# A gate of a decoder layer by seven products of quarters, its combined weights by adding DMAs, its products summed in the PSUM banks

## The chip, the cores and the metric

The kernel runs on one core of a Trainium2 chip. A core has TensorE (PE, matmuls), VectorE (DVE), ScalarE (ACT), GpSimd (POOL), SyncE (SP, which here only issues DMAs) and 16 DMA engines between the chip's memory (HBM) and the core's on-chip memory (SBUF). Matmuls write into PSUM, of which the kernel uses eight banks. The metric is the time of one execution on the device in microseconds (us).

## The reference, cut to what matters

One decoder layer on 512 tokens of 1024 features, fp32. With `u = rmsnorm(x)`, one wide product gives everything that the token mixer needs:

```
proj = u @ w_in                      # 512 x 1024 times 1024 x 10128
q, k, v, pool_in, z, xbc, dt_raw, gate_pre = split(proj)
y_a = dilated_attention(q, k, v) @ w_a        # 3 groups of 6 heads
y_b = pool_mixer(pool_in) @ w_b
y_c = ssd_mixer(z, xbc, dt_raw) @ w_c
gates = sigmoid(gate_pre + b_gate)            # 3 gates of 1024
x = x + (gates0 * y_a + gates1 * y_b + gates2 * y_c) @ w_o
x = x + conv_ffn(rmsnorm(x))
return rmsnorm(x)
```

The change is about the second gate (`gates1`, 1024 columns of `w_in`), about the columns of V for the attention groups 1 and 2 (384 each), and about those of Q and K for group 1 (384 each).

## The kernel before, in words

**Products.** Every fp32 factor is split into a high and a low part, and a product is three matmuls: high x high, high x low, low x high (`mm3`, L229; the matmul is L237, and in it the parts with the low weights come last). `u` lies in SBUF as `uh` and `ul`, with features on the partitions. A `Job` is one tile of weights: its raw tile is loaded by SP (`fetch`, L183), ScalarE copies it to the high part in two halves (`cast`, L196), VectorE subtracts to get the low part (`low`, L216), and TensorE multiplies (the job's body). High parts have three buffers, low parts two, raw tiles two.

**Order.** The program is a list of jobs with calls between them (`program`, L1504 to L1565). PE, ACT, DVE and POOL run their instructions in the order in which the program writes them; SP's are placed by the scheduler as soon as their buffers allow. At the start of job n the main loop writes: the low part of job n+1, then (if that job has one) its `then`, the cast of n+2 (put on a list, `second`, that is worked off at the job's last `step()` and behind its body), the load of n+3, and then the body of n. A `step()` also moves on the side works (`running`, `waiting`), attention above all, by one piece.

**Plain groups.** `gate_jobs(b)` makes a gate of eight chunks of 128 features: each has 24 matmuls of 512 columns into one bank, a sigmoid on ScalarE (L1226), and for gate 1 a product with the branch's output on VectorE (L1228). Two chunks are a job with a raw tile of 1 MB.

**Groups of seven.** A product of a 2 x 2 matrix of quarters by another such takes eight products of quarters, or seven of combined quarters (a scheme of Strassen's kind). `sums_of_u` (L403) makes the four combined quarters of `u` (VectorE and ScalarE); `side_u` hands out a quarter or a combination. `sevens` (L344) is such a group for V of groups 1 and 2, `qk_sevens` (L700) for Q and K of group 1: seven jobs of quarters of 768 KB. Four quarters of weights are loaded (two by `fetch`, two into tiles `w3` of the pool `ypool`, which has two buffers), and VectorE makes the combined ones by differences in place (`diff`, L341; each runs behind a low part). Each product has two banks of its own; partial results are copied out by ScalarE (L370, L735) and summed by VectorE (L375, L378, L383, L662, L745).

**The stretch.** The order is: pool input jobs, V and Q, K of group 0, attention of group 0 (as side work), the eight chunks of `w_b` with all four `sums_of_u` from its third job on, four chunks of gate 1, the seven products of V, the seven of Q and K, attention of group 1 (side work), the other four chunks of gate 1, twelve chunks of XBC (whose convolution is done behind each), the state-space part, and so on to the FFN, which has two groups of seven of its own (`down_group`) and ends with the norm.

**Other buffers.** General tiles of 2 KB per partition come from the pool `big` with NBIG = 54 buffers. The row of norm factors (`grow`, L444) has a pool of its own (4 KB per partition).

Of the kernel before, what the change touches and what calls it, by code (L numbers as in the profile page):

```python
# [82 lines left out]
def trunk(ctx: ExitStack, tc, out, x, rel_bias, ln1_g, w_in, b_gate, w_a, pool_w, pool_scale, w_b,  # L83
# [10 lines left out]
    rows = ctx.enter_context(tc.tile_pool(name="rows", bufs=1))  # L94
# [5 lines left out]
    ypool = ctx.enter_context(tc.tile_pool(name="ypool", bufs=2))  # L100
# [221 lines left out]
    def sums_of(f0, f1, ah, al, found):  # L322


        sa, sb = T("sa"), T("sb")
        dve.tensor_tensor(sa[:, LO], f0[:, HI], f1[:, HI], OP.add)
        dve.tensor_tensor(sa[:, HI], sa[:, LO], f0[:, LO], OP.subtract)
        dve.tensor_tensor(sb[:, LO], f0[:, LO], f0[:, HI], OP.subtract)
        dve.tensor_tensor(sb[:, HI], f1[:, LO], sa[:, HI], OP.subtract)
# [13 lines left out]

    def sevens(quarter, c, side, W, emit):  # L344

        r1, r2, r3, r5 = {}, {}, {}, {}

        def job(j, load, form, use):  # L350
            def body(ws):
                wh, wl = ws
                parts = side(j)
                for i in range(2):
                    ps = MM("pb")
                    o = slice(i * P, (i + 1) * P)
                    mm3(ps[:, :c], lambda k: wh[:, k, :], lambda k: wl[:, k, :],
                        lambda k: parts[k][0][:, o], lambda k: parts[k][1][:, o], range(4), flip=True)
                    use(i, ps[:, :c])
                step()  # L360
            new = Job([load] if load is not None else [], 4, c, body)
            new.form = form
            if load is None:
                new.load = lambda: None
            return new

        def keep(r, name):
            def use(i, ps):
                r[i] = T(name)[:, :c]
                act.copy(r[i], ps)  # L370
            return use

        def p5(i, ps):
            keep(r5, "r5")(i, ps)
            dve.tensor_tensor(r2[i], r2[i], ps, OP.add)  # L375

        def p6(i, ps):
            dve.tensor_tensor(r1[i], r1[i], ps, OP.add)  # L378
            emit(0, 1, i, r1[i], r2[i])

        def p7(i, ps):
            r3[i] = T("r3")[:, :c]
            dve.tensor_tensor(r3[i], r1[i], ps, OP.add)  # L383
            emit(1, 1, i, r3[i], r5[i])

        one = job("A11", quarter(0, 0), None, keep(r1, "r1"))
        two = job("A12", quarter(1, 0), None, lambda i, ps: emit(0, 0, i, r1[i], ps))
        three = job(4, None, lambda: W[1], keep(r2, "r2"))
        one.then = lambda: diff(one.raw, W[0], one.raw)
        three.then = lambda: diff(W[0], W[1], W[0])  # L390
        two.then = lambda: diff(W[1], W[1], one.raw)
        yield one
        yield three
        yield two
        yield job(1, None, lambda: one.raw, p5)
        yield job(2, None, lambda: W[1], p6)
        yield job(3, None, lambda: W[0], p7)
        yield job("A22", None, lambda: diff(two.raw, two.raw, W[1]),
                  lambda i, ps: emit(1, 0, i, r3[i], ps))
# [3 lines left out]
    def sums_of_u(p):  # L403

        f = []
        for k in (2 * p, 2 * p + 1):
# [4 lines left out]
                           lambda j, h, l: US.__setitem__((j, p), (h, l)))  # L411
# [32 lines left out]
    def grow(src):  # L444
        g = rows.tile([P, D], F32, name="grow", tag="grow")
        sp.dma_start(g, src.partition_broadcast(P))
        return g
# [11 lines left out]
    def norm_early(t, g):  # L459
# [4 lines left out]
        pool.tensor_tensor(xg, t, g[:, :S], OP.mult)  # L464
# [3 lines left out]
    def norm_late(t, g, v0, outs, last=None):  # L468
# [6 lines left out]
        dve.tensor_tensor(xg, t, g[:, S:], OP.mult)  # L475
# [171 lines left out]
    def v_pair():  # L647

        c, W = C_V + 384, []
        vd = dram.tile([S, 384], F32, name="vdram")  # L650
        rows_ = lambda c0: w_in[:, c0:c0 + 384].rearrange("(k two p) c -> two p k c", two=2, p=P)
        quarter = lambda two, h: rows_(c + 384 * h)[two]

        def load():
            for two in range(2):
                W.append(ypool.tile([P, 4, S], F32, name="w3", tag="xs")[:, :, :384])
                sp.dma_start(W[two], quarter(two, 1))

        def emit(hi, right, i, a, ps):
            g, tb = 1 + right, 2 * hi + i  # L660
            t = T(f"v{g}")
            dve.tensor_tensor(t[:, :384], a, ps, OP.add)  # L662
            if g == 2:
                sp.dma_start(vd[tb * P:(tb + 1) * P, :], t[:, :384])
                return

            for n in range(4):
                if (g, n) not in V:
                    V[g, n] = T(f"vr{g}")
                sp.dma_start(V[g, n][32 * tb:32 * tb + 32, :384], t[n:P:4, :384])  # L670
# [8 lines left out]
        return load, sevens(quarter, 384, side_u, W, emit), residues  # L679
# [20 lines left out]
    def qk_sevens(g):  # L700


        W = []
# [3 lines left out]
        r1, r2, r3, r5 = {}, {}, {}, {}  # L707

        def load():
            for two in range(2):  # L710
                W.append(ypool.tile([P, 4, S], F32, name="w3", tag="xs")[:, :, :384])
                sp.dma_start(W[two], quarter(two, 1))

        def job(j, raw, form, use):
            def body(ws):
                wh, wl = ws
                parts = side_u(j)
                for i, ms in enumerate(chunks):
                    ps = MM("pq")
                    for n, m in enumerate(ms):  # L720
                        o = slice(m * P, (m + 1) * P)
                        mm3(ps[:, 256 * n:256 * n + 256], lambda k: wh[:, k, o], lambda k: wl[:, k, o],
                            lambda k: parts[k][0], lambda k: parts[k][1], range(4))
                    use(i, ps[:, :256 * len(ms)])
                step()
            new = Job([raw] if raw is not None else [], 4, 384, body)
            new.form = form
            if raw is None:
                new.load = lambda: None
            return new  # L730

        def keep(r):
            def use(i, ps):
                r[i] = T("rq")[:, :ps.shape[-1]]
                act.copy(r[i], ps)  # L735
            return use

        def emit(which, hi, i, a, b):

            for n, m in enumerate(chunks[i]):  # L740
                if (which, g, m) not in QK:
                    QK[which, g, m] = T(f"{which}{g}")
                view = (grouped if which == "q" else plain)(QK[which, g, m], g)
                piece = lambda t: perm(t[:, 256 * n:256 * n + 256], g)
                dve.tensor_tensor(view[:, :, 64 * hi:64 * hi + 64], piece(a), piece(b), OP.add)  # L745

        def p5(i, ps):
            keep(r5)(i, ps)
            dve.tensor_tensor(r2[i], r2[i], ps, OP.add)

        def later(i):
            emit("k", 0, i, r1[i], r2[i])
# [3 lines left out]
        def p6(i, ps):  # L756
            dve.tensor_tensor(r1[i], r1[i], ps, OP.add)
            running.append(after(1, later(i)))

        def p7(i, ps):  # L760
            r3[i] = T("rq")[:, :ps.shape[-1]]
            dve.tensor_tensor(r3[i], r1[i], ps, OP.add)
            emit("k", 1, i, r3[i], r5[i])

        one = job("A11", quarter(0, 0), None, keep(r1))
        two = job("A12", quarter(1, 0), None, lambda i, ps: emit("q", 0, i, r1[i], ps))
        three = job(4, None, lambda: W[1], keep(r2))
        one.then = lambda: diff(one.raw, W[0], one.raw)
        three.then = lambda: diff(W[0], W[1], W[0])
        two.then = lambda: diff(W[1], W[1], one.raw)  # L770
        return load, [one, three, two, job(1, None, lambda: one.raw, p5), job(2, None, lambda: W[1], p6),
                      job(3, None, lambda: W[0], p7), job("A22", None, lambda: diff(two.raw, two.raw, W[1]),
                                                          lambda i, ps: emit("q", 1, i, r3[i], ps))]

# [729 lines left out]
    def program():  # L1504
        yield from jobs_a(w_in, C_POOL, 8, uhk, ulk, KD, pool_evac)
        yield Call(lambda: waiting.append(rows_of_bias()))
        yield from v_jobs(0)
        yield from qk_jobs(0)
        yield from pool_out_job()
        yield Call(lambda: attend(0))  # L1510
        yield Call(lambda: waiting.insert(3, ssd_prep()))
        for i, job in enumerate(branch_jobs(1, w_b, YB, 8, more=range(7))):
# [3 lines left out]
        load, pair, residues_of_v = v_pair()  # L1516
        yield Call(load)
        yield from gate_jobs(1, 0, SPLIT)
# [267 lines left out]
```

## Time and profile before

| what | value |
|---|---|
| three runs | 1023.89 to 1024.44 us, median 1024.22 |
| the profiled execution | 1024.13 us |
| its span in the profile | 1022.4 us |
| granted TensorE clock | 0.999 |
| bytes moved | 118.08 MB, 115 GB/s over the span |

The profile is of one execution; its own time is 1.73 us more than its span. In the lines below, L237 is a line of the kernel, `pa`, `pb`, `pq` are names of PSUM tiles (`pa` a chunk of a gate, of XBC, of w_b; `pb` V; `pq` Q and K of group 1), `wh` and `wl` high and low parts of weights, `raw` and `w` raw weights. "x24" is a count. A group's row gives the total in us and the mean of one in ns, and then how long the engine was idle just before and what ended that.

### The profile page before, as it was taken

The numbers are of one execution on the slowest core, as the hardware profiler recorded it, in microseconds if no ns is written. First come the engines' busy times: TensorE is split into PE (matmuls) and PEld (weight loads), VectorE is DVE, ScalarE is ACT, GpSimd is POOL, SyncE is SP. The second block draws the span as 40 slices with busy tenths as digits, with TensorE's granted clock in tenths as the row PEclk, the third lists the DMA queues.
The fourth block names the chain that finished last, engine by engine and source line by source line (L and its number), as shares of the span: only waits on it lengthen the run. The fifth ranks groups of instructions, "written<-read, shape, count | busy, mean of one in ns | idle before, by whom it ended". The sixth has DMA issues, their size and how long they took to land.

```text
span 1022.4 us, 13249 instructions
## 1 busy us (share of the span) xinstructions
PE 1013.1 (99%) x5258; PEld 857.6 (84%) x5258; DVE 701.4 (69%) x890; ACT 507.9 (50%) x847; POOL 127.2 (12%) x108
## 2 busy tenths in 40 slices
PE   8999999999999999999999999999999999999997
PEld 8998878899888888888888888898888888888886
DVE  6563566788766656676879666768778768685756
ACT  5432545454574366878567224554444434433434
POOL 1770000000000000000044501102111100111002
PEclk9999999999999999999999999999999999999999
DMA  8444312124442354552254526542232333321322
GB/s 269 138 118 135 105 62 76 31 83 145 124 118 83 87 151 112 145 138 74 79 140 160 165 83 237 178 142 86 94 113 83 99 107 122 126 83 42 124 83 82
DMA packets 114077, 118.08 MB, mean 115 GB/s; under 512 B 6212, under 2 KB 97927, under 8 KB 114016
## 3 DMA queue, kind: packets, MB, share of 16 engines
q1 hardware_dynamic: 113423, 116.39, 37.0%
q8 instruction: 41, 0.67, 0.3%
q10 hardware_dynamic: 592, 0.86, 0.3%
q14 instruction: 21, 0.16, 0.1%
HBM read 113.44 MB, written 3.00 MB: 114 GB/s over the span
## 4 chain that ended last, share of the span: by engine, by line
PE 98%; DMA 1%; DVE 0%; ACT 0%; ACTq 0%; issue 0%
PE pa L237 36%; PE pu L237 22%; PE pb L237 12%; PE pd L237 7%; PE pqk L237 6%; PE pq L237 3%; PE pa L1633 2%; PE ps L799 1%; PE pu L1434 1%; PE ppw L237 1%; PE po L847 1%; PE pt L833 1%; PE py L1132 1%; DMA xin<-in_x_dram 1%; PE pyo L1139 1%; PE pst L1120 0%
## 5 line engine op out<-in xcount | busy, mean ns | idle before, releaser
L216 DVE TENSOR_TENSOR wl<-raw,wh 128x2048 fp32r<-128x2048 f32 (+3 forms) x95 | 220.1, 2318 | 47.5 <-ACT wh L196 39.7
L196 ACT CAST wh<-raw 128x1024 fp32r<-128x1024 f32 (+4 forms) x187 | 186.5, 1017 | 42.7 <-DVE raw L341 18.0
L1329 DVE SCALAR_TENSOR_TENSOR hc<-pu,fcol,hc 128x510 f32<-128x510 f32 x88 | 65.9, 748 | 56.4 <-ACT hc L1326 54.8
L237 PE MATMUL pa<-uh,wh 128*128 128x512 f32 x384 | 97.0, 395 | 0.0
L237 PE MATMUL pa<-ul,wh 128*128 128x512 f32 x384 | 94.9, 389 | 0.0
L237 PE MATMUL pa<-uh,wl 128*128 128x512 f32 x384 | 94.8, 389 | 0.0
L237 PEld LDWEIGHTS pa<-ul,wh 128*128 128x128 f32 x384 | 72.1, 188 | 15.1
L237 PEld LDWEIGHTS pa<-uh,wl 128*128 128x128 f32 x384 | 72.1, 188 | 14.9
L237 PE MATMUL pu<-uh,wh 128*128 128x512 f32 (+1 forms) x352 | 83.5, 379 | 0.0
L237 PE MATMUL pu<-uh,wl 128*128 128x512 f32 (+1 forms) x352 | 83.5, 379 | 0.0
L237 PE MATMUL pu<-ul,wh 128*128 128x512 f32 (+1 forms) x352 | 83.5, 379 | 0.0
L237 PEld LDWEIGHTS pa<-uh,wh 128*128 128x128 f32 x384 | 70.6, 188 | 14.3
L237 PEld LDWEIGHTS pu<-uh,wl 128*128 128x128 f32 x352 | 64.2, 188 | 12.5
L237 PEld LDWEIGHTS pu<-ul,wh 128*128 128x128 f32 x352 | 64.2, 188 | 12.4
L237 PEld LDWEIGHTS pu<-uh,wh 128*128 128x128 f32 x352 | 64.1, 188 | 12.4
L1326 ACT ACTIVATE hc<-pu,fcol,fcol 128x512 f32<-128x512 f32 x40 | 31.2, 779 | 78.9 <-PE pu L237 78.9
L1334 POOL TENSOR_TENSOR hc<-hc 128x512 f32<-128x512 f32 x22 | 30.8, 1401 | 289.0 <-DVE hc L1329 252.0
L1115 POOL TENSOR_TENSOR st<-st,dts 128x512 f32<-128x512 f32 x4 | 4.5, 1126 | 380.4 <-ACT st L1123 322.0
L821 ACT ACTIVATE sb<-sb,nmls 128x128 f32<-128x128 f32 (+1 forms) x72 | 30.0, 418 | 25.7 <-DVE nmls L818 13.6
L1331 ACT ACTIVATE hc<-hc 128x512 f32<-128x512 f32 x22 | 13.9, 632 | 39.9 <-DVE hc L1329 39.9
L1226 ACT ACTIVATE sg<-pa,col 128x512 f32<-128x512 f32 x24 | 16.5, 689 | 32.1 <-PE pa L237 31.0
L969 DVE SCALAR_TENSOR_TENSOR xs<-pa,col,xs 128x509 f32<-128x509 f32 (+2 forms) x24 | 18.0, 749 | 17.1 <-ACT xs L965 16.6
(393 smaller groups left out, 1872.6 us busy)
## 6 DMA issues: line engine op xcount, KB each, us to landing
raw<-in_w_in_dram SPq DMA_DIRECT2D x25, 1024.0 KB, 5.2
raw<-in_ffn_w_up_dram SPq DMA_DIRECT2D x22, 1024.0 KB, 5.1
raw<-in_w_o_dram SPq DMA_DIRECT2D x8, 1024.0 KB
raw<-in_ffn_w_down_dram SPq DMA_DIRECT2D x8, 1024.0 KB, 5.1
raw<-in_w_in_dram SPq DMA_DIRECT2D x14, 512.0 KB, 4.8
raw<-in_w_in_dram SPq DMA_DIRECT2D x6, 768.0 KB, 4.6
raw<-in_w_b_dram SPq DMA_DIRECT2D x4, 1024.0 KB, 5.1
al<-ad SPq DMA_DIRECT2D x16, 256.0 KB, 7.3
```

The lines of the kernel that those rows point to most:

```text
L196: (other.tensor_copy if other and i else act.copy)(job.high[:, :, o], job.raw[:, :, o])
L216: (eng or dve).tensor_tensor(l[:, :, o], job.raw[:, :, o], h[:, :, o].bitcast(F32), OP.subtract)
L237: pe.matmul(ps, l, r, start=first and n == 0, stop=last and n == total - 1, skip_group_check=onto)
L799: pe.matmul(pss[i][:, o:o + w * P], q[r, n * P:(n + 1) * P], k[r, kb * P:(kb + w) * P], start=True, stop=True)
L821: act.activation(sb[:, off:off + w * P], sb[:, off:off + w * P], AF.Exp, bias=nm[:, n, h:h + 1], accum_out=ls[:, n, h:h + 1])
L969: dve.scalar_tensor_tensor(t[:, sh:], ps[:, :S - sh], col[:, o_cw + 12 * k + m:o_cw + 12 * k + m + 1], t[:, sh:], OP.mult, OP.add)
L1226: act.activation(s, ps, AF.Sigmoid, bias=col[:, o:o + 1])
L1326: act.activation(t, ps, AF.Identity, bias=ff["c1"][:, ff["b"] + m:ff["b"] + m + 1], scale=fw(2, m))
L1329: dve.scalar_tensor_tensor(t[:, sh:], ps[:, :S - sh], fw(k, m), t[:, sh:], OP.mult, OP.add)
L1331: act.activation(t, t, AF.Silu)
L1334: pool.tensor_tensor(a, a, t, OP.mult)
L1633: pe.matmul(first[2 * n + j][:, lo:hi], a[:, k, j * P:(j + 1) * P], b[:, k, lo:hi], start=a is wh and b is uh and k == 0, stop=a is wl and ...
```

## The change

1. *The second gate by seven products.* `gate_jobs(1)` is replaced by `gate_seven(1)`: four quarters of 512 x 512 weights (1 MB each), seven products, each of four chunks of 128 features by 256 tokens. Its seven stand in front of those of V. `SPLIT` goes.
2. *One class for the three groups.* `Seven` replaces `sevens` and the body of `qk_sevens`. Order of a group: two, (the last product, four, of the group before), five, three, one, six, seven; four follows behind the next group's two, or behind the first XBC job.
3. *Combined weights by adding DMAs.* Two tiles W0 and W1 per group are loaded by SP. `plus` adds another quarter onto one of them by two DMAs from GpSimd (`accum_op=OP.add`), each of two of the four blocks of 128 rows: 512 KB in the gate, 384 KB in the others. There are four `plus` per group: one after the load (W0), and one behind the low part of five (W0), of three (W1) and of six (W0). VectorE's differences in these groups go.
4. *Products add up in their banks.* Three adds onto the two banks of five; six, seven and four onto those of one. After each product its banks are read: copied out by ScalarE (two, five, three), or added to or subtracted from a kept copy by VectorE (one, six, seven), or read as they are (four). In the gate, a sigmoid on ScalarE follows for each chunk of 256 columns, and a product with the branch's output on VectorE.
5. *Signs.* The scheme needs another sign in one combination of `u` (`turned`).
6. *Places.* `sums_of_u`: two of the four in the Q, K jobs of group 0, two from the third w_b job on. The gate's first tile is loaded ahead of the second w_b job, its second ahead of the third. Attention of group 1 begins behind the first XBC job and Q, K's four.
7. *Memory.* `ypool` three buffers for two, `big` 52 for 54; the row of norm factors is two tiles of `big`, and its pool goes.

The diff, cut to its core:

```diff
+    class Seven:
+        def __init__(self, quarter, c, widths, product, done, name):
+            R, A, B, W = {}, [], [], [None, None]
+            def tile_of(i):
+                W[i] = ypool.tile([P, 4, S], F32, name="w3", tag="xs")[:, :, :c]
+                sp.dma_start(W[i], quarter(i, 1))
+            def plus(i, two, h):
+                for k in (0, 2):
+                    pool.dma_start(W[i][:, k:k + 2, :], quarter(two, h)[:, k:k + 2, :], accum_op=OP.add)
+            def job(j, raw, form, bank, use, more=False):
+                def body(ws):
+                    if not more:
+                        bank[:] = [MM(name) for _ in range(2)]
+                    for i in range(2):
+                        product(bank[i], ws, side_u(j), i, more)
+                        use(i, bank[i][:, :widths[i]])
+                    step()
...
+            self.two = job("A12", quarter(1, 0), None, B, keep(0, 0))
+            five = job(1, None, lambda: W[0], B, keep(1, 1))
+            three = job(4, None, lambda: W[1], B, keep(0, 1), True)
+            one = job("A11", quarter(0, 0), None, A, end(0, 0, OP.add))
+            six = job(2, None, lambda: W[0], A, end(0, 1, OP.subtract), True)
+            seven = job(3, None, lambda: W[1], A, end(1, 1, OP.subtract), True)
+            self.four = job("A22", None, lambda: W[0], A, end(1, 0), True)
+            five.then = lambda: plus(0, 1, 1)
+            three.then = lambda: plus(1, 0, 1)
+            six.then = lambda: plus(0, 1, 0)
+            self.jobs = five, three, one, six, seven
+            self.load = lambda: tile_of(0), lambda: plus(0, 0, 0), lambda: tile_of(1)
...
+    def by_features(chunks):
+        def product(ps, ws, parts, i, more):
+            for n, m in enumerate(chunks[i]):
+                o = slice(m * P, (m + 1) * P)
+                mm3(ps[:, 256 * n:256 * n + 256], lambda k: ws[0][:, k, o], lambda k: ws[1][:, k, o],
+                    lambda k: parts[k][0], lambda k: parts[k][1], range(4), onto=more or n > 0)
+        return product
...
+    def gate_seven(b):
...
+        def done(hi, right, i, r, ps, op):
+            if r is not None:
+                dve.tensor_tensor(r, r, ps, op)
+            for n, m in enumerate(chunks[i]):
+                m += 4 * right
...
+                act.activation(SG[b, m][:, 256 * hi:256 * hi + 256],
+                               (ps if r is None else r)[:, 256 * n:256 * n + 256],
+                               AF.Sigmoid, bias=col[:, o:o + 1])
+                if hi:
+                    running.append(after(1, total(m)))
...
-            if i == 3:
-                yield Call(lambda: running.extend(after(p, sums_of_u(p)) for p in range(4)))
+            if i == 1:
+                yield Call(gates.load[0])
+            if i == 2:
+                yield Call(lambda: running.extend(after(2 * p - 4, sums_of_u(p)) for p in (2, 3)))
+                yield Call(gates.load[1])
+                yield Call(gates.load[2])
             yield job
...
+        last = None
+        for group, next_ in zip(groups, groups[1:] + (None,)):
+            yield group.two
+            if last:
+                yield last.four
+            last = group
+            for i, job in enumerate(group.jobs):
+                if next_ and i >= 2:
+                    yield Call(next_.load[i - 2])
+                yield job
+        xbc = jobs_a(w_in, C_XBC, 12, uhk, ulk, KD, xbc_evac)
+        yield next(xbc)
+        yield last.four
         yield Call(lambda: attend(1))
```

More of the change, by code (lines that the diff above doesn't have):

```diff
@@ L342, in diff @@
         return out
[L344 to L399, printed above, removed]
@@ new lines, in trunk, with keep, use, end @@
+    class Seven:
[15 more added lines that the diff above has]
+                    step()
+                new = Job([raw] if raw is not None else [], 4, c, body)
+                new.form = form
+                if raw is None:
+                    new.load = lambda: None
+                return new
+            def keep(hi, right):
+                def use(i, ps):
+                    r = R[hi, right, i] = T("r7")[:, :widths[i]]
+                    act.copy(r, ps)
+                return use
+            def end(hi, right, op=None):
+                return lambda i, ps: done(hi, right, i, R.get((hi, right, i)), ps, op)
+            self.two = job("A12", quarter(1, 0), None, B, keep(0, 0))
[10 more added lines that the diff above has]
+            self.load = lambda: tile_of(0), lambda: plus(0, 0, 0), lambda: tile_of(1)
@@ L647, in v_pair @@
     def v_pair():
-        c, W = C_V + 384, []
+        c = C_V + 384
         vd = dram.tile([S, 384], F32, name="vdram")
[L651 to L659, printed above, removed]
-            g, tb = 1 + right, 2 * hi + i
-            t = T(f"v{g}")
-            dve.tensor_tensor(t[:, :384], a, ps, OP.add)
+        def product(ps, ws, parts, i, more):
+            o = slice(i * P, (i + 1) * P)
+            mm3(ps[:, :384], lambda k: ws[0][:, k, :], lambda k: ws[1][:, k, :],
+                lambda k: parts[k][0][:, o], lambda k: parts[k][1][:, o], range(4), flip=True, onto=more)
+        def done(hi, right, i, r, ps, op):
+            g, tb = 1 + right, 2 * hi + i
+            if r is None:
+                r = T(f"v{g}")[:, :384]
+                act.copy(r, ps)
+            else:
+                dve.tensor_tensor(r, r, ps, op)
             if g == 2:
-                sp.dma_start(vd[tb * P:(tb + 1) * P, :], t[:, :384])
+                sp.dma_start(vd[tb * P:(tb + 1) * P, :], r)
                 return
@@ L706, in qk_sevens, with done @@
         chunks = ((0, 1), (2,))
[L707 to L738, printed above, removed]
+        def done(hi, right, i, r, ps, op):
+            which = "qk"[right]
             for n, m in enumerate(chunks[i]):
@@ L742, in emit @@
                     QK[which, g, m] = T(f"{which}{g}")
-                view = (grouped if which == "q" else plain)(QK[which, g, m], g)
+                view = (plain if right else grouped)(QK[which, g, m], g)[:, :, 64 * hi:64 * hi + 64]
                 piece = lambda t: perm(t[:, 256 * n:256 * n + 256], g)
[L745 to L749, printed above, removed]
@@ L751, in later, with total @@
-        def later(i):
-            emit("k", 0, i, r1[i], r2[i])
+                if r is None:
+                    dve.tensor_copy(view, piece(ps))
+                else:
+                    dve.tensor_tensor(view, piece(r), piece(ps), op)
+        return Seven(quarter, 384, (512, 256), by_features(chunks), done, "pq")
+    def gate_seven(b):
+        quarter = lambda two, h: w_in[:, C_GATE + b * D + S * h:C_GATE + b * D + S * h + S].rearrange(
+            "(k two p) c -> two p k c", two=2, p=P)[two]
+        chunks = ((0, 1), (2, 3))
+        def total(m):
+            dve.tensor_tensor(MG[m], MG[m], SG[b, m], OP.mult)
@@ L753, in later @@
             return
             yield
[L756 to L773, printed above, removed]
+        def done(hi, right, i, r, ps, op):
+            if r is not None:
+                dve.tensor_tensor(r, r, ps, op)
+            for n, m in enumerate(chunks[i]):
+                m += 4 * right
+                if (b, m) not in SG:
+                    SG[b, m] = T("sg")
+                o = o_bg + 8 * b + m
+                act.activation(SG[b, m][:, 256 * hi:256 * hi + 256],
[3 more added lines that the diff above has]
+                    running.append(after(1, total(m)))
@@ L775, in attend @@
+        return Seven(quarter, S, (512, 512), by_features(chunks), done, "pa")
     def attend(g):
```

48 lines of the change are left out of this document (22 added, 26 removed).

## The prediction

> **What bounds the kernel now.** First the page's totals and its chain of waits, to see which engine sets the end.
>
> ```profile
> span 1022.4 us, 13249 instructions
> PE 1013.1 (99%) x5258; PEld 857.6 (84%) x5258; DVE 701.4 (69%) x890; ACT 507.9 (50%) x847; POOL 127.2 (12%) x108
> PE 98%; DMA 1%; DVE 0%; ACT 0%; ACTq 0%; issue 0%
> ```
>
> TensorE works in 99% of the span and 98% of the chain is TensorE. So time falls only where matmul time falls, and any moment for which TensorE waits is added in full. Next the pieces of the chain around the change (start, length, what; both in us).
>
> ```profile
> 188.44 16.34 PE pa L237 x72
> 204.77 29.14 PE pb L237 x168
> 233.92 30.23 PE pq L237 x252
> 264.15 5.46 PE pa L237 x24
> 270.71 11.11 PE pa L237 x48
> 323.29 38.10 PE pa L237 x168
> ```
>
> The first and the fourth and fifth are gate chunks (24 matmuls of 512 columns each), the last is XBC, `pb` is the second and third V, `pq` is Q and K of group 1. Between these stand only pieces of attention: no gap. The table by stretches (PE, PEld, DVE, ACT, POOL busy; granted clock; share of the DMA engines; GB/s) shows what is free beside them:
>
> ```profile
> 20.00:30.00 10.00, 9.86 (x85) 9.69 (x84) 5.75 (x16) 4.02 (x10) 0.00 (x0) 1.00 1.07 369
> 204.80:233.90 29.10, 29.10 (x170) 29.10 (x170) 24.52 (x25) 13.53 (x21) 0.00 (x0) 1.00 0.39 117
> 233.90:264.10 30.20, 30.20 (x254) 30.20 (x253) 26.22 (x28) 13.48 (x20) 0.00 (x0) 1.00 0.34 110
> ```
>
> In both groups of seven the clock is full, VectorE is busy for 84 to 87%, GpSimd does nothing, and the DMA engines are two thirds idle. Now the groups of operations, shapes kept apart, from 125 to 290 us (busy us, mean ns of one):
>
> ```profile
> L216 DVE TENSOR_TENSOR wl<-raw,wh 128x2048 fp32r<-128x2048 f32 x7 | 16.0, 2283 | 1.0 <-ACT sb L821 1.0
> L196 ACT CAST wh<-raw 128x1024 fp32r<-128x1024 f32 x14 | 14.5, 1046 | 7.0 <-DMA raw<-in_w_in_dram 7.0
> L216 DVE TENSOR_TENSOR wl<-w,wh 128x1536 fp32r<-128x1536 f32 x6 | 10.5, 1753 | 2.0 <-ACT wh L196 2.0
> L196 ACT CAST wh<-w 128x768 fp32r<-128x768 f32 x12 | 9.5, 832 | 3.6 <-DMA w<-in_w_in_dram 3.6
> L1226 ACT ACTIVATE sg<-pa,col 128x512 f32<-128x512 f32 x8 | 5.5, 689 | 15.6 <-PE pa L237 15.5
> L1228 DVE TENSOR_TENSOR yo<-yo,sg 128x512 f32<-128x512 f32 x7 | 4.8, 692 | 15.6 <-ACT sg L1226 15.5
> L341 DVE TENSOR_TENSOR w<-w,w 128x1536 f32<-128x1536 f32 x2 | 3.5, 1753 | 0.0
> L745 DVE TENSOR_TENSOR q<-rq,pq 128x256 f32<-128x256 f32 x6 | 3.3, 608 | 0.0
> L370 ACT COPY r<-pb 128x384 f32<-128x384 f32 x6 | 2.9, 482 | 8.4 <-PE pb L237 8.3
> L735 ACT COPY rq<-pq 128x512 f32<-128x512 f32 x3 | 1.8, 588 | 6.6 <-PE pq L237 6.6
> L735 ACT COPY rq<-pq 128x256 f32<-128x256 f32 x3 | 1.1, 373 | 2.6 <-PE pq L237 2.6
> L375 DVE TENSOR_TENSOR r<-r,pb 128x384 f32<-128x384 f32 x2 | 1.1, 554 | 1.8 <-ACT r L370 1.8
> L326 DVE TENSOR_TENSOR sa<-uf 128x256 f32<-128x256 f32 x4 | 1.7, 418 | 0.0
> ```
>
> and the page's DMA issues (KB each, us from issue to landing); none was issued by GpSimd, none adds:
>
> ```profile
> raw<-in_w_in_dram SPq DMA_DIRECT2D x25, 1024.0 KB, 5.2
> raw<-in_w_in_dram SPq DMA_DIRECT2D x6, 768.0 KB, 4.6
> al<-ad SPq DMA_DIRECT2D x16, 256.0 KB, 7.3
> ```
>
> **The change, part by part.**
>
> 1. *Matmuls of the gate.* Removed are 8 chunks; three of them took 16.34, so one 5.45 and eight 43.57. Added are 7 products of 48 matmuls of 256 columns. The `pq` piece has that shape: 30.23 / 252 = 0.120 each, 336 of them 40.31 (5.76 a product). TensorE saves **3.26 us**. V and the Q, K group keep 168 and 252 matmuls: 0. A product there lasts 29.14 / 7 = 4.16 and 30.23 / 7 = 4.32. This is the only gain that I find, and so about its ceiling.
>
> 2. *Products that add up in their banks.* Before, every product had a bank of its own. Now three adds onto five's bank, and six, seven and four follow one another in one's. The next product cannot begin until the copy or sum of the partial result in its first bank has been read. That read stands in VectorE's or ScalarE's order behind the preparation of a later job, and so does this chain arise: end of product n, evacuation of its second bank, cast of n+2 (ScalarE, two halves), low part of n+2 (VectorE), evacuation of n+1's first bank, start of n+2. It has the length of product n+1 to hide in. Handovers between engines, estimated from this piece of the timeline (cast 209.37 + 1.57 = 210.94, VectorE starts at 210.98), are 0.04 to 0.06; four make 0.2.
>
> ```profile
> 209.37 1.57 ACT L196 CAST wh<-raw 128x768 fp32r<-128x768 f32 x2
> 210.98 1.76 DVE L216 TENSOR_TENSOR wl<-raw,wh 128x1536 fp32r<-128x1536 f32 x1 [0.21 <-ACT wh L196]
> ```
>
>  - Gate, before six: copy 0.59 + cast 2.09 + low 2.28 + sum 0.69 + 0.2 = 5.85 against 5.76: 0.1.
>  - Gate, before seven: sum 0.69, then two sigmoids of 256 columns. No row has that form; 0.373 (the copy of 256) is a lower and 0.689 (the sigmoid of 512) an upper bound, and scaled as the copies are, 0.689 x 373 / 588 = 0.44. 0.69 + 0.87 + 2.09 + 2.28 + 0.69 + 0.2 = 6.82 against 5.86 (product six and the 0.1 before it): 1.0.
>  - Gate's four stands behind V's first product, of 4.16, and needs its low part 8 matmuls (0.96) after its own start: 0.69 + 0.87 + 2.09 + 2.28 + 0.2 = 6.13 against 5.12: 1.0.
>  - V, before six: copy 0.48 + cast 1.66 + low 1.75 + sum 0.55 + 0.2 = 4.64 against 4.16: 0.5.
>  - Q, K, before six: copy 0.37 + 1.66 + 1.75 + two pieces of q at 0.61 + 0.2 = 5.20 against 4.32: 0.9; if a piece costs 0.42, as the plain sums of 256 columns do (L326), 0.5. I take 0.6.
>  - The others have time: before seven of V, ScalarE has nothing to evacuate after product one, so the cast is early.
>
>  Together **3.2** (2.8 to 3.5). With every row a little shorter beside idle neighbours it could be 1.3; below nothing it cannot be, since none of these waits is in the kernel before.
>
> 3. *Weights combined by adding DMAs.* Removed from VectorE: 8 differences of 1.75, 14 us in the two groups, and some of the sums. None of it was on the chain, so it gains 0; it makes the chains of part 2 no worse. Added: 24 adding transfers on GpSimd's queue, in pairs of 384 KB (V, Q and K) or 512 KB (gate). What is queued behind them on GpSimd: nothing but each other, by the zeros of the table. Each pair is issued when the low part of the tile's former use is done, and must have landed at the cast of its next use. From the product lengths: the low part of five is done some 4 us into gate's four, so the pair for V's six has 1.8 + 2 x 4.16 = 10.1; that for seven is issued about 2.2 into five and has 3 x 4.16 - 2.2 = 10.3; that for four has 8.4, and then 2 more, since its own job stands one product further off. So each has **about 10 us**; in the gate 12.8 to 16.
>  What one costs, no row shows. Lower bound: the plain 768 KB, 4.6. Upper bound, far off: `al` at 7.3 for 256 KB, 21.9 for 768. Adding means reading the old tile and the new quarter, so I reckon with up to twice the plain one, 9.2, and take 7: in time, 0. The DMA engines have room for that: four pairs of 768 KB in V's 29.1 us are 108 GB/s, by the first row of the table (1.07 at 369) a share of 0.31, so 0.39 becomes 0.70; at half the rate it becomes 1.01, just full. If the cover is gone, each microsecond over 10 is paid up to six times (six, seven, four, in two groups).
>
> 4. *What is moved.* Two of the four sums of u go to the Q, K jobs of group 0 and two to the w_b jobs: same work, VectorE has room in both, 0; not more than 1 if it hasn't. Attention of group 1 now runs beside the XBC jobs alone instead of four gate chunks and XBC; TensorE's work is the same and XBC lasts to 323.29 + 38.10 = 361.39: 0. At the start, SP issues 0.72 MB more ahead of the third weight tile; at 369 GB/s that is 2 us later. Its cast starts without idle time right behind another ScalarE instruction:
>
> ```profile
> 31.25 1.07 ACT L918 COPY pu<-pa 128x512 f32<-128x512 f32 x2 [5.72 <-PE pa L1633]
> 32.21 1.91 ACT L196 CAST wh<-raw 128x2048 fp32r<-128x2048 f32 x1
> ```
>
>  So ScalarE and not the transfer sets it: 0; 2 us, once, if the cover is too short. The factors of the last norm (512 KB) now go just ahead of the last weights; their cast would start some 1.4 later (512 KB at 369 GB/s), but the low part that follows does not run before 1000.53: 0, at most 1.4.
>
> ```profile
> 993.79 1.14 ACT L196 CAST wh<-raw 128x512 fp32r<-128x512 f32 x2 [4.08 <-DMA raw<-in_ffn_w_down_dram]
> 1000.53 1.94 DVE L216 TENSOR_TENSOR wl<-raw,wh 128x1024 fp32r<-128x1024 f32 x1
> ```
>
> **The sum.** The profiled execution took 1024.13: 1022.4 of span and 1.73 around it. 1024.13 - 3.26 + 3.2 = 1024.07. I forecast **1024.1**, no change that counts. The median of the three runs, 1024.22, is 0.09 above the profiled one. 0.2% of it, about what a measurement of this kernel can tell from no change, is 2.05: below 1022.2 is faster, above 1026.3 slower.
>
> **The rivals.**
>
>  - *A, the chains hide.* The evacuations in the first bank are done earlier, or VectorE and ScalarE run them quicker; at most 1.3 of stalls stay. For: VectorE loses 14 us of differences and is less often late. Against: the chains hold no difference, only casts and low parts, whose rows are steady. Time: 1024.13 - 3.26 + 0 to 1.3 = 1020.9 to 1022.2; its middle 1021.5.
>  - *C, the adding transfers land late.* Mechanism: a pair takes longer than it has between low part and cast, ScalarE waits at the cast, VectorE behind it, TensorE at the bank. For a single pair it decides from 10 us on; the price is up to 6 us for each further one. At 11: 1024.1 + 6 = 1030.1. At 21.9, the far bound: 1024.1 + 71 = 1095, which I give 3%. It can decide earlier where two pairs share the queue: that for four and the first of the next group are issued close together, in the job of product one, and the second of them has 0.1 + 2 x 4.16 + 4.32 = 12.7. At twice the plain transfer, 2 x 9.2 = 18.4, it is 5.7 late, 2.6 of which lie under V's four (4.16 less the cast of 1.66 that product five needs first): 3.1 once, 1027.2. For C: two reads per byte and one queue that no row prices. Against: 4.6 for the plain transfer and a share of 0.70 where the plain rate holds.
>  The Trainium skill, Collectives: The Full Stack, section "The bandwidth ceiling: the fold count and why AG ≠ RS ≠ AR", says that a reduction moves at half the rate of a copy, because the add reads two sources on one ring. That is the doubled transfer of C; no run shows it yet.
>  - *D, the change does not save its matmuls*: adding onto a bank costs more than 0.120 a matmul. The `pq` rows already add 12 matmuls into one region at that price, so I give it 2%; at 0.130 it would be 1024.1 + 3.4 = 1027.5.
>
> **How the numbers follow.** Forecast (stalls eat the gain, 1023.0 to 1025.5): 0.37. A: 0.27. C: 0.34 with its far end. D: 0.02. Faster is A and a sliver of the forecast, 0.28; slower is C and D, 0.36; the same is the rest, 0.36. The range starts at 1020.8, just under the floor of A, and goes to 1032, which is C at 11.3 us; what is left out is C beyond that, some 0.15, and little below. The likeliest case alone is 1023.0 to 1025.5.
>
> **What would show it.** Right if the gate's 336 matmuls take 40.3, if TensorE is idle for about 1 us before the gate's seven and in its four and 0.5 before the sixes of V and of Q, K, with VectorE or ScalarE as releaser, and if no cast waits for a GpSimd transfer. A shows as no such gaps. C shows as ScalarE idle at L195's casts with a DMA as releaser, and gaps of a microsecond or more at six products. It would be wrong in kind if gaps appear outside 125 to 290 us, at the start or in the w_b jobs.

## The result, and the profile after

| | before | after |
|---|---|---|
| median of 5 runs, us | 1024.24 (1023.89 to 1024.96) | 1065.08 (1063.38 to 1066.91) |
| profiled execution, us | 1024.13 | 1065.05 |
| its span, us | 1022.4 | 1063.3 |
| granted TensorE clock | 0.999 | 0.985 |

The ratio is 1.040, with a 95% interval of 1.0384 to 1.0415: 40.8 us slower. I forecast 1024.1, and the range ended at 1032.

The page of the changed kernel, its parts 1, 4, 3 and 6:

```profile
span 1063.3 us, 13629 instructions
PE 1024.3 (96%) x5402; PEld 873.7 (82%) x5402; DVE 691.2 (65%) x877; ACT 511.5 (48%) x863; POOL 153.1 (14%) x132
PE 89%; issue 5%; DMA 2%; DVE 1%; POOL 1%; ACT 1%; ACTq 0%; DVEq 0%; POOLq 0%
q0 software_dynamic: 6528, 10.49, 6.5%
w<-in_w_in_dram POOLq DMA_DIRECT2D x16, 384.0 KB, 5.3
w<-in_w_in_dram POOLq DMA_DIRECT2D x8, 512.0 KB, 5.8
```

TensorE went from 99 to 96% of a longer span, and the chain now has a tenth that is not TensorE: "issue", POOL and DMA. A new queue, `q0`, carries the 24 adding transfers. One by one they are quick: 5.3 and 5.8 us from issue to landing. Their stretch in the table by windows (PE, PEld, DVE, ACT, POOL busy; granted clock; DMA share; GB/s):

```profile
182.30:223.00 40.70, 40.00 (x338) 39.37 (x338) 18.11 (x14) 21.61 (x34) 8.47 (x7) 1.00 0.68 136
223.00:257.50 34.50, 27.61 (x152) 26.60 (x150) 15.07 (x15) 11.01 (x19) 6.09 (x5) 0.90 0.59 114
257.50:333.00 75.50, 54.39 (x313) 51.57 (x314) 27.07 (x26) 20.94 (x30) 12.18 (x10) 0.84 0.59 126
```

The gate's products (first row) hardly suffer. Then TensorE is idle for 6.9 us of 34.5 and for 21.1 of 75.5, and where it works its clock is lower. The DMA engines are not full (0.59), so they are not what is short. GpSimd's timeline in this stretch (start, length, what, idle time before and what ended it) shows what is:

```profile
184.71 1.21 POOL L356 DMA_DIRECT2D w<-in_w_in_dram  x1 [100.40 <-DVE wl L215]
190.82 1.22 POOL L356 DMA_DIRECT2D w<-in_w_in_dram  x1 [4.89 <-issue]
196.91 1.20 POOL L356 DMA_DIRECT2D w<-in_w_in_dram  x1 [4.88 <-issue]
202.78 1.21 POOL L356 DMA_DIRECT2D w<-in_w_in_dram  x1 [4.66 <-issue]
...
260.02 1.22 POOL L356 DMA_DIRECT2D w<-in_w_in_dram  x1 [4.39 <-issue]
265.51 1.22 POOL L356 DMA_DIRECT2D w<-in_w_in_dram  x1 [4.27 <-issue]
```

The first two are the halves of one pair. Nothing in the program stands between them, and yet the second is issued 6.11 us after the first; those of 384 KB follow one another at 5.49 in the pair shown last and at 5.6 further on. That is the time to landing (5.8, 5.3) and 0.2 to 0.3 more: **one adding transfer at a time**, and between them GpSimd waits, as a rule, for nothing that the profile shows ("issue"). 22 of them lie between 184.71 and the last landing, about 322: 137 us, while the matmuls of these groups, with the pieces of attention and XBC between them, fill some 113 (40.3 + 29.1 + 30.2, 10.9 of XBC and 2.2 of attention). What waits is ScalarE at its casts and behind it TensorE; from the table of waits (total us, times, longest):

```profile
POOL w L356 <- issue: 75.5, 16, 6.1
ACT wh L195 <- DMA w<-in_w_in_dram: 59.2, 8, 10.7
PE pb L236 <- DVE r L657: 8.6, 2, 6.3
```

TensorE's waits of over 2 us stand ahead of the products five, six and seven of V (3.67, 2.38 and 6.26) and of Q, K (5.62, 3.41 and 5.37).

The lower clock is the other part of the loss, about a third of it. TensorE's timeline behind a gap, each row four matmuls of V:

```profile
234.82 1.29 PE L236 MATMUL pb<-wh,sah 128*128 128x384 f32 x4 [3.67 <-ACT wh L195]
235.91 1.48 PE L236 MATMUL pb<-wh,sal 128*128 128x384 f32 x4
237.19 1.48 PE L236 MATMUL pb<-wl,sah 128*128 128x384 f32 x4
...
239.28 0.85 PE L236 MATMUL pb<-wh,sal 128*128 128x384 f32 x4
```

After 3.67 us of waiting a row of four takes up to 1.48 instead of 0.85, for about 4 us. Over the whole kernel TensorE is busy for 1024.3 us; in e1 below, with the same matmuls, for 1010.9. The spans differ by 38.9 us (1063.3 and 1024.4): 13.4 of them are slower matmuls and the other 25.5 idle time.

### The profile page after: what moved, and what is told of

The parts are those of the page before. It is cut to its first block, busy times and chain, and to the rows that moved or that the text cites. A ratio compares the mean times of both kernels' runs of the same rounds, so it can differ in the third digit from the quotient of the medians.

```text
span 1063.3 us, 13629 instructions
## 1 busy us (share of the span) xinstructions
PE 1024.3 (96%) x5402; PEld 873.7 (82%) x5402; DVE 691.2 (65%) x877; ACT 511.5 (48%) x863; POOL 153.1 (14%) x132
## 3 DMA queue, kind: packets, MB, share of 16 engines
q0 software_dynamic: 6528, 10.49, 6.5%
## 4 chain that ended last, share of the span: by engine, by line
PE 89%; issue 5%; DMA 2%; DVE 1%; POOL 1%; ACT 1%; ACTq 0%; DVEq 0%; POOLq 0%
PE pa L236 33%; PE pu L236 22%; PE pb L236 9%; PE pd L236 7%; PE pqk L236 6%; PE pa L1620 2%; DMA w<-in_w_in_dram 2%; PE pq L236 1%; PE ps L775 1%; PE pu L1410 1%; PE po L823 1%; POOL w L356 1%; PE ppw L236 1%; PE pt L809 1%; PE py L1108 1%
## 5 line engine op out<-in xcount | busy, mean ns | idle before, releaser
L215 DVE TENSOR_TENSOR wl<-raw,wh 128x2048 fp32r<-128x2048 f32 (+3 forms) x89 | 208.4, 2342 | 58.4 <-ACT wh L195 50.6
L195 ACT CAST wh<-raw 128x1024 fp32r<-128x1024 f32 (+4 forms) x175 | 176.2, 1025 | 32.5 <-DMA raw<-in_ffn_w_down_dram 12.4
L236 PE MATMUL pa<-uh,wh 128*128 128x512 f32 (+1 forms) x368 | 88.8, 381 | 0.0
L236 PE MATMUL pa<-uh,wl 128*128 128x512 f32 (+1 forms) x368 | 86.9, 375 | 0.8 <-DVE wl L215 0.8
L236 PE MATMUL pa<-ul,wh 128*128 128x512 f32 (+1 forms) x368 | 86.8, 375 | 0.0
L215 DVE TENSOR_TENSOR wl<-w,wh 128x2048 fp32r<-128x2048 f32 (+1 forms) x21 | 43.8, 2087 | 59.2 <-ACT wh L195 53.0
L236 PEld LDWEIGHTS pa<-uh,wl 128*128 128x128 f32 x368 | 66.7, 188 | 13.5 <-DVE wl L215 1.0
L236 PEld LDWEIGHTS pa<-ul,wh 128*128 128x128 f32 x368 | 66.7, 188 | 12.6
L195 ACT CAST wh<-w 128x1024 fp32r<-128x1024 f32 (+1 forms) x42 | 38.1, 944 | 61.6 <-DMA w<-in_w_in_dram 59.2
L356 POOL DMA_DIRECT2D w<-in_w_in_dram x24 | 29.3, 1222 | 215.8 <-DVE wl L215 117.4
```

Source lines behind the costliest of these rows:

```text
L195: (other.tensor_copy if other and i else act.copy)(job.high[:, :, o], job.raw[:, :, o])
L215: (eng or dve).tensor_tensor(l[:, :, o], job.raw[:, :, o], h[:, :, o].bitcast(F32), OP.subtract)
L236: pe.matmul(ps, l, r, start=first and n == 0, stop=last and n == total - 1, skip_group_check=onto)
L356: pool.dma_start(W[i][:, k:k + 2, :], quarter(two, h)[:, k:k + 2, :], accum_op=OP.add)
```

## The experiments

Theory R: GpSimd's queue has a ring for its descriptors, whose size stands in the launch line of the kernel (`dynamic_dma_scratch_size=1024`, in both kernels); one adding half leaves no room for a second. Rival S: adding transfers, or transfers of this queue, go one at a time whatever the ring. Rival T: something else in the change (sums in the banks, moved work, fewer tiles).

**e1, no adding, SP's queue.**

```diff
-                    pool.dma_start(W[i][:, k:k + 2, :], quarter(two, h)[:, k:k + 2, :], accum_op=OP.add)
+                    sp.dma_start(W[i][:, k:k + 2, :], quarter(two, h)[:, k:k + 2, :])
```

> Each pair of adding transfers is replaced by a pair of plain ones of the same size on SP's queue; the weights are then not combined (the tile holds one quarter instead of a sum), all else of the change is kept. Theory R (GpSimd's queue holds up the adding transfers, since its ring of descriptors, 1024 bytes in the launch line, has no room for a second one): the 40 us go, and what stays is the 3.3 us of matmuls saved against the gate's short waits (0.1, 0.7 and 0.8 in the changed kernel's trace) and those of V and Q, K that my prediction gave 0.5 and 0.6: 1022 to 1025 us. Theory S (adding transfers run one at a time whatever the ring): the same. Theory T (sums in the banks, moved attention or tighter buffers cost the time): 1050 us or more.

Measured: 1026.82 us, ratio 1.0019 (1.0008 to 1.0030). T is out as the cause of the 40 us. But e1 is 1.8 above the 1022 to 1025 that I expected, and not faster than before. The TensorE waits that are left behind the start, from the table of waits:

```profile
PE pa L236 <- DVE wl L215: 0.8, 1, 0.8
PE po L823 <- ACT sb L810: 0.8, 1, 0.8
PE pa L236 <- DVE r L737: 0.7, 1, 0.7
PE pq L236 <- DVE q L721: 0.6, 1, 0.6
PE pb L236 <- ACT wh L195: 0.2, 1, 0.2
```

Four of the five are waits that the prediction named, at their places; the one for `sb` lies in the w_b jobs. The chain of waits gives two landmarks, the first product of the gate and the transposition ahead of the FFN. Before:

```profile
180.74 5.47 PE pa L237 x24
...
645.71 1.75 PE uT L453 x16
```

and e1:

```profile
182.40 5.74 PE pa L236 x48
190.37 11.53 PE pa L236 x96
...
647.69 1.75 PE uT L447 x16
```

Between the landmarks before takes 464.97, e1 465.29. The 3.26 of saved matmuls (96 of them take 11.53, so 0.120 each, as predicted) have turned into 0.3 of loss: 3.6 us of waits, as a difference. The table above lists 2.3 of them in the groups. It counts from the ends of matmuls, which are modelled; counted by how much later than usual TensorE's rows start in e1, the same four places cost 1.1 (gate's four), 0.9 (gate's seven), 0.8 (Q, K's six) and 0.5 (V's six), and the gate's six 0.2: together 3.5. The other 1.7 of the span's 2.0 lie ahead of the gate: 0.4 at the start and 1.24 in the w_b jobs (from their first whole chunk, 124.59 and 125.01, to the gate 56.15 and 57.39).

**e2, no adding, GpSimd's queue.**

```diff
-                    pool.dma_start(W[i][:, k:k + 2, :], quarter(two, h)[:, k:k + 2, :], accum_op=OP.add)
+                    pool.dma_start(W[i][:, k:k + 2, :], quarter(two, h)[:, k:k + 2, :])
```

> The same plain transfers, but issued by GpSimd as in the changed kernel (weights not combined). R: a plain one needs one read per row instead of two, so more than one fits into the ring; the next is issued about 1.2 us after the last instead of 5.5 to 6.1, and the time falls to 1022 to 1030 us. S, if it is the adding that forbids two at a time: the same. S, if it is GpSimd's queue as such that takes one at a time: a period of over 5 us again, and 1055 us or more.

Measured: 1026.73 us, ratio 1.0021 (1.0010 to 1.0032), the same as e1 within the intervals. GpSimd's timeline, and its queue and transfers on the page:

```profile
207.46 2.17 POOL L356 DMA_DIRECT2D w<-in_w_in_dram  x3 [11.29 <-DVE wl L215]
212.65 0.72 POOL L356 DMA_DIRECT2D w<-in_w_in_dram  x1 [3.02 <-issue]
```

```profile
q0 software_dynamic: 2944, 10.49, 3.1%
w<-in_w_in_dram POOLq DMA_DIRECT2D x16, 384.0 KB, 3.9
```

Three are issued in one go, 0.72 each; only the fourth waits. So the queue does not take one at a time. S is left only as a property of adding. And plain transfers of the same 10.49 MB take 3.1% of the DMA engines, adding ones 6.5%.

**e3, a larger ring.**

```diff
-NBIG = 52
+NBIG = 50
-    nc = _bacc.Bacc("TRN2", target_bir_lowering=False, num_devices=1, dynamic_dma_scratch_size=1024)
+    nc = _bacc.Bacc("TRN2", target_bir_lowering=False, num_devices=1, dynamic_dma_scratch_size=4096)
```

> The changed kernel with a ring of 4096 bytes instead of 1024 (the launch line), paid for by two general tiles (50 instead of 52). R: the second of a pair is issued 1.2 us after the first, a pair lands in 7 to 9 us, and the time is 1021 to 1030 us. S: the period stays at 5.5 to 6.1 and the time at 1060 to 1068 us. T: no change either, or slower for want of tiles.

Measured: 1039.6 us, ratio 1.0136 (1.0118 to 1.0154). GpSimd's timeline, and then TensorE's waits:

```profile
188.89 2.43 POOL L356 DMA_DIRECT2D w<-in_w_in_dram  x2 [114.03 <-DVE wl L215]
210.91 4.92 POOL L356 DMA_DIRECT2D w<-in_w_in_dram  x4 [10.32 <-DVE wl L215]
```

```profile
PE po L823 <- ACT sb L810: 3.8, 1, 3.8
PE pxs L1063 <- DVE o L828: 2.2, 1, 2.2
PE po L823 <- DVE sbt L804: 1.3, 1, 1.3
```

Both halves of a pair, and four transfers where two pairs meet, are issued back to back: S is out. No wait of V's or Q, K's groups is longer than 0.5. The time misses the expected 1021 to 1030 by 10 us: the waits that are left belong to attention and the state-space part, where before has none. They speak for the two tiles that paid for the ring; e5 asks that.

**e4, smaller transfers in the small ring.**

```diff
-                for k in (0, 2):
-                    pool.dma_start(W[i][:, k:k + 2, :], quarter(two, h)[:, k:k + 2, :], accum_op=OP.add)
+                for k in range(4):
+                    pool.dma_start(W[i][:, k:k + 1, :], quarter(two, h)[:, k:k + 1, :], accum_op=OP.add)
```

> The changed kernel with four adding transfers of one block of 128 rows each (192 or 256 KB) instead of two of two blocks, ring as it is. R: each needs half as many descriptors, so that two or three are under way at once; a tile takes 7 to 9 us instead of 11 to 12, and the time falls to 1025 to 1045 us. S: each still waits for the one before, with a period of 4 us or more, so a tile takes 16 us or more and the time rises to 1090 us or more.

Measured: 1039.51 us, ratio 1.0140 (1.0123 to 1.0157). GpSimd's timeline and TensorE's waits:

```profile
184.95 2.63 POOL L356 DMA_DIRECT2D w<-in_w_in_dram  x3 [102.90 <-DVE wl L215]
189.17 0.88 POOL L356 DMA_DIRECT2D w<-in_w_in_dram  x1 [1.59 <-issue]
```

```profile
PE pb L236 <- DVE r L657: 4.6, 2, 4.4
PE pq L236 <- DVE k L721: 4.0, 1, 4.0
```

Twice as many transfers, 26 us faster than the changed kernel: three fit at a time, the fourth waits. R holds with the ring unchanged. Two waits of over 4 us are left, which e6, with a larger ring, does not have.

**e5, the tiles alone.** e1 with `NBIG = 50`.

> Run e1 (plain transfers on SP's queue, weights not combined, ring of 1024) with 50 general tiles instead of 52. It asks what the 15 us are that were left in the run with the larger ring. If they are the two missing tiles (there ScalarE and VectorE had to wait for buffers, outside the three groups): the same waits without any adding transfer, 1036 to 1042 us against 1026.8 with 52. If they are the adding transfers themselves (two reads, more load on the DMA engines): it stays at 1026 to 1028 us.

Measured: 1037.91 us, ratio 1.0133 (1.0117 to 1.0148). TensorE's waits:

```profile
PE po L823 <- ACT sb L810: 3.8, 1, 3.8
PE pxs L1063 <- DVE o L828: 2.2, 1, 2.2
PE po L823 <- DVE sbt L804: 1.3, 1, 1.3
```

The same three waits as in e3, to the tenth, without any adding: two tiles of 2 KB cost 11 us, and explain nearly all that was left in e3.

**e6, a ring of 2048 with 52 tiles.** The kilobyte comes from constants of the state-space part:

```diff
-        xx, t, u, s, zz, dtv, a = (f(nme) for nme in ("dtx", "dtt", "dtu", "dts", "dtz", "dtv", "dta"))
-        dve.tensor_tensor(v4(xx), dtr, bc(0), OP.add)
+        t, u, s, zz, dtv = (f(nme) for nme in ("dtt", "dtu", "dts", "dtz", "dtv"))
+        a = t
+        xx = dtr.rearrange("p a b -> p (a b)")
+        dve.tensor_tensor(dtr, dtr, bc(0), OP.add)
-        acs, tot, dec = (f(nme) for nme in ("acs", "dts", "dtz"))
+        acs, tot, dec = (f(nme) for nme in ("dtu", "dts", "dtz"))
+        cst["acs"] = acs
-    nc = _bacc.Bacc("TRN2", target_bir_lowering=False, num_devices=1, dynamic_dma_scratch_size=1024)
+    nc = _bacc.Bacc("TRN2", target_bir_lowering=False, num_devices=1, dynamic_dma_scratch_size=2048)
```

> The changed kernel with a ring of 2048 bytes and all 52 tiles; the kilobyte comes from small constants of the state-space part that now share tiles (two temporaries reused, one sum in place). R: three halves fit into the ring instead of one, so the second of a pair is issued 1.2 us after the first, no cast in V's and Q, K's groups waits for an adding transfer, and the time is that of the plain transfers, 1025 to 1028 us. If adding slows other transfers or is itself too slow at three at a time: 1030 us or more.

Measured: 1027.83 us (its profiled run 1026.73), ratio 1.0040 (1.0029 to 1.0050). GpSimd's timeline, and its transfers on the page:

```profile
207.44 3.68 POOL L356 DMA_DIRECT2D w<-in_w_in_dram  x3 [10.29 <-DVE wl L215]
213.46 1.20 POOL L356 DMA_DIRECT2D w<-in_w_in_dram  x1 [2.34 <-issue]
```

```profile
w<-in_w_in_dram POOLq DMA_DIRECT2D x16, 384.0 KB, 6.8
```

Three halves go back to back and the fourth waits. TensorE's waits behind the start are those of e1, none over 0.8. With the weights combined, one kilobyte of ring takes the changed kernel from 1065.1 to 1027.8: 37 of the 41 us. Between the landmarks it takes 465.27, as e1 does (465.29); its median is 1.0 above that of e1, and its span in the profile 0.5. One thing did not come as expected: casts of V's and Q, K's groups still wait for adding transfers, 14.6 us at four casts (the longest 6.39), but TensorE is not held up by it. So ScalarE idle at a cast is not by itself a sign of loss.

**e7, casts ahead.** e6, and

```diff
                         use(i, bank[i][:, :widths[i]])
+                    while second:
+                        flush()
                     step()
...
-            three = job(4, None, lambda: W[1], B, keep(0, 1), True)
+            three = job(4, None, lambda: W[1], B, keep(0, 1, True), True)
...
+                if r is None:
+                    sigmoid()
+                else:
+                    running.append(once(sigmoid))
```

(`keep(..., True)` puts the copy of the second bank behind the casts in the same way; `once` calls what it is given at the `step()`.)

> e6, and in the three groups ScalarE's casts stand ahead of what only reads kept tiles (the gate's sigmoids) or a bank that no product adds onto any more (the copy of three's second bank). It asks for the chains that my prediction priced at 3.2 us and that measured 3.5 in e1: without sigmoids and copies in them the gate's waits (2.1) and those of V and Q, K (1.4) fall to 0.5 to 1.2 together, and the time by 2 to 3 us from e6, to 1022.5 to 1025.5. If the chains do not set the end: within 0.5 us of e6.

Measured: 1023.15 us, ratio 0.9995 (0.9986 to 1.0004). Between the landmarks 645.43 - 182.32 = 463.11, 2.2 less than e6 (648.02 - 182.75 = 465.27). TensorE's waits in the groups are now

```profile
PE pq L241 <- DVE k L731: 0.5, 1, 0.5
PE pq L241 <- DVE q L731: 0.5, 1, 0.5
```

The gate's two and V's one are gone, as expected; one for k is new. The medians differ by 4.7, more than the 2.2 to 2.6 of the profiles (1026.73 and 1024.13); the runs of e6 scatter up to 1030.46, and I go by the profiles.

**e8, sums of u one step later.** e7, and

```diff
-                yield Call(lambda: running.extend(after(2 * p - 4, sums_of_u(p)) for p in (2, 3)))
+                yield Call(lambda: running.extend(after(2 * p - 3, sums_of_u(p)) for p in (2, 3)))
```

> e7 with the last two sums of u one step later. In e1 TensorE lost 1.2 us in the w_b jobs, where a ScalarE operation waited 3.2 us for a buffer; if the early sums hold the tiles that it lacks, this goes and the time is 0.8 to 1.2 us below e7, so 1021.5 to 1024.5. If the buffer is held by something else: as e7, or later sums hold up the first product that needs them by up to 1.5 us.

Measured: 1022.52 us, ratio 0.9987 (0.9977 to 0.9997). The chain of waits has the first whole w_b chunk, the gate and the transposition at

```profile
124.71 5.66 PE pa L241 x24
...
180.86 5.74 PE pa L241 x48
...
643.51 1.75 PE uT L457 x16
```

From w_b to the gate it takes 56.15, just as before, where e7 takes 57.38. The ScalarE operation that was late, in e7 and then in e8:

```profile
166.90 0.59 ACT L1031 ACTIVATE east<-pact 16x512 f32<-16x512 f32 x1 [3.23 <-PE po L837]
163.33 0.59 ACT L1031 ACTIVATE east<-pact 16x512 f32<-16x512 f32 x1 [0.95 <-DVE acst L1028]
```

In e7 it waits for a matmul `po`, which makes none of its data: for a tile to come free. In e8 it waits for its own data alone. So the early sums did hold the buffers. Between the landmarks e8 takes 462.65, 2.3 less than before; of the 3.26 saved, some 1 us still goes in waits (0.6 of it one wait for q, in the table of waits). Its median is 0.6 below that of e7, and 1.6 below before (1022.52 against 1024.12). That is 0.13%, and the interval ends just short of 1: at most a small gain. The changed kernel is beaten by over 40 us.

## Why the prediction was wrong

- **Part 3, the adding transfers: the step that failed.** It priced one pair by its bytes, 7 us, up to 9.2 and 21.9 as a far bound, and gave every pair a window of its own of about 10. The pair's bytes were priced well: where both halves are under way (e6) a half lands after 6.8 and a pair takes about 1.2 + 6.8 = 8.0. But it took for granted that both halves are under way at once. In the changed kernel they run one behind the other, 5.5 + 5.3 = 10.8, and so do all pairs: four in V's 29 us need 44. "What is queued behind them on GpSimd: nothing but each other" was true, and I added up the bytes of four pairs but not their times. That alone would not have shown it: at my price four pairs are 28 us and just fit, at 9.2 they are 37 and do not. The ring, which forbids two, stands in the launch line and is not in the prediction at all.
- **Rival C** named the right thing, late adding transfers, and the right order of waits (ScalarE at the cast, VectorE, TensorE at the bank). It also named six products; they are five, six and seven of two groups, not six, seven and four. Its price was too small. At 10.8 its rule, 6 us for each one over 10, gives some 5 and not 38, since lateness of a full queue adds up from pair to pair, and since TensorE runs slower behind each long wait (a granted clock of 0.90 and 0.84 in the two windows, some 13 us), which the rule left out. (In its sum for two pairs on the queue, 4.16 less 1.66 is 2.5 and not 2.6; nothing hangs on it.)
- The rule of the Trainium skill that stood beside C (Collectives: The Full Stack, section "The bandwidth ceiling: the fold count and why AG ≠ RS ≠ AR") agrees with the runs: adding took 6.1 to 6.5% of the DMA engines (e6: 6.2), plain transfers of the same bytes 3.1% (e2). It is not what cost the time.
- **Part 1** was right: 0.120 a matmul, so D is out, and 3.26 us of TensorE's work are gone.
- **Part 2** was right, in size and in place: 3.2 predicted, 3.6 measured in e1. For the gate's six, seven and four, V's six and Q, K's six it had 0.1, 1.0, 1.0, 0.5 and 0.6; they cost 0.2, 0.9, 1.1, 0.5 and 0.8. A is out, for this order; e7, which moves sigmoids and copies behind the casts, saves 2.2 of it.
- **Part 4** was 0 and measured 1.24 in the w_b jobs: VectorE had room, as I said, but the early sums held general tiles, and a ScalarE operation waited for one (e8 against e7). The end cost nothing: behind the second landmark before and e1 both take 376.7. I priced the moved sums in engine time alone. Two fewer general tiles in the change were not priced either; that two fewer again cost 11 us (e5) says how near the edge the pool stands. The start (0.4 in e1, 0.1 in e8) is not told apart from the scatter of the first loads.
- Where the ring does not hold it up, the change is at 1027.8 (e6), and at 1026.8 with nothing added (e1): within the range, 2.7 to 3.7 above the point, of which 1.24 are the sums.

## What to carry to other kernels

Before work is handed to a queue that has stood idle, add up all that it will carry and ask how many items can be under way at once; a time to landing, however good, does not tell it. Here a queue that ran one item at a time showed "issue" gaps that made its period an item's own time to landing and a little more; a larger ring (e6) and smaller items (e4) both helped. When a change moves work earlier, price the buffers that it holds and not only the engine that does it.

## What the runs showed of the hardware

- The ring in bytes: at 1024 one adding half at a time (after), at 2048 three (e6); plain halves (e2) and adding blocks of half that size (e4) three at 1024. So, worked out on the premise that the whole ring can be filled, an adding half takes more than 512 and at most 682 bytes of it, and a plain half at most 341.
- Adding takes about twice the DMA engines' time, 6.2 against 3.1% (e6, e2). The Trainium skill, DMA: Bandwidth & Descriptors, says in its section "Terms" that a descriptor has 16 bytes and that this queue's stand in rings in on-chip memory, and in "The descriptor swizzle" that in its example each engine has, on the read and on the write side, one descriptor more than its data needs. By that, an estimate: if the 1024 bytes are the ring of one engine, they are 64 descriptors, and an adding half of 256 rows is 16 rows per engine, with two reads each 32, and one more: 33, of which 64 hold one and 128 hold three. That agrees with the runs; no run counts descriptors. The profile counts packets: 6528 for the 24 adding halves, 272 each, which is 256 rows and 16 more; second reads do not show in it.
- An issue on GpSimd takes 1.2 us for an adding half, 0.88 for an adding block, 0.72 for a plain half.
- In the changed kernel TensorE went on at full speed after waits of 0.70 and 0.83 us; after those of 2.38 to 6.26 us it was slower for 3 to 6 us, at V's products 1.48 for what takes 0.85.
